# Attention in a hybrid DeltaNet and windowed-attention layer: softmax scaling moved into the transposition of the probabilities

## The chip, the cores and the metric

The kernel runs on one core of one Trainium2 chip. The core has five engines that run side by side, each working through its own queue of instructions in order: PE (TensorE, matmuls; its weight loads are shown as PEld), DVE (VectorE), ACT (ScalarE), POOL (GpSimd) and SP (SyncE, which here only issues DMAs). The metric is the time of one execution on the device in microseconds (us).

## What is computed

One layer of a diffusion backbone over 2048 latent tokens and 256 context tokens, model width 1024. One projection of the normalised, modulated input feeds two mixers: a bidirectional gated DeltaNet in chunks, and an attention over a window of |i-j| <= 128 plus all context keys. Both are gated, projected, merged by sigmoid gates and projected once more. Only the attention is touched by the change:

```python
s_loc = einsum('bnqhgd,bnkhd->bhgnqk', qb, kw) * scale      # window: 3 blocks of 128 keys
s_loc = where(valid, s_loc, NEG_INF)
s_ctx = einsum('bnqhgd,bkhd->bhgnqk', qb, kc) * scale       # 256 context keys
p = softmax(concatenate([s_loc, s_ctx, sink_l], axis=-1), axis=-1)
o = (einsum('bhgnqk,bnkhd->bnqhgd', p[..., :nloc], vw)
     + einsum('bhgnqk,bkhd->bnqhgd', p[..., nloc:nloc + nctx], vc))
```

There are 8 query heads in 2 groups of 4; each group shares one key and value head of width 64. `sink_l` is one logit per head that counts in the denominator alone. All inputs and outputs are fp32.

## The kernel before

**Stages.** The kernel works in stages that overlap at their borders: modulation and normalisation, the projections with the short convolution (up to about 640 us), the gates with the triangular solves, the DeltaNet scan with gate products beside it (about 900 to 1320 us), the attention (about 1340 to 1768 us), and the last projection (to the end). A matmul whose operands need fp32 accuracy is mostly written as three products of rounded `fp32r` parts, high by high, low by high, high by low (lines 535 to 537 for the gates, 1247 to 1249 for the projections of both branches, `pps`). The scan multiplies plain fp32 operands instead (line 1115 is one of its products).

**Attention.** It works in 32 units. A unit is one block of 128 queries (16 blocks) and one group of four heads (2 groups). Its window has three blocks of keys (two for the first and the last block) and two blocks of context keys, so a unit has five (or four) key blocks.

- `scores` (lines 926 to 941): for each of four heads two products with the window's keys (high and low part, 384 columns) and two with the context's (256 columns) into the PSUM tile `sc`; one DVE operation (line 933) adds the band mask, scales, and writes the negated scores `pr` [128 queries x 640 keys] and the row's extreme into `sm[:, h, 1]`; ACT (line 935) takes the exponential in place and sums it into `sm[:, h, 2]`. Then the denominator of all four heads at once, on 128x4 elements: DVE add (937), ACT exponential (938), DVE add, doubling and reciprocal (939 to 941) into `sm[:, h, 3]`. POOL multiplies each head's 640 probabilities by its reciprocal (943), in place. (The doubling belongs to the gate that follows, which is kept at twice its value.)
- `weighted` (lines 948 to 970): for each key block four transpositions (957) of a head's 128x128 piece into one PSUM tile `pt`; ACT rounds it to `ph` (959), DVE takes the rest `pl` (961), and PE adds both products with the values into `av` (963, 964). At the end ACT and DVE join the halves of `av` (967, 968), POOL multiplies with the gate `szb` (969), and SP stores it.

`sc` and `pt` have two buffers each in PSUM, `av` has one; `pr` and `sm` have three.

**What sets the order.** The code names operations in program order; a scheduler then simulates the queues with costs of its own and fixes each engine's order before the run. `scores` of a unit is named two units ahead of its `weighted` (`AHEAD = 2`). Beside the attention, with less priority, come the last gate products (`rps`, lines 535 to 537) and then, not before the units that they need are done (`paced`), the projections `pps` of three of four groups of 512 tokens. Each such product consists of 12 matmuls for one branch; DVE multiplies it by its gate (`ta`, `tb`, line 1258), POOL adds the two (1263). After the last unit the last projection follows in an order written out by hand.

Of the kernel before, what the change touches and what calls it, by code (L numbers as in the profile page):

```python
# [7 lines left out]
F32 = mybir.dt.float32  # L8
# [3 lines left out]
ALU = mybir.AluOpType  # L12
# [16 lines left out]
def f32(ap):  # L29
    return ap.bitcast(F32)  # L30


def hybrid(tc, ins, out, dbg=None, upto=9):
    nc = tc.nc
    V, S, G, T = nc.vector, nc.scalar, nc.gpsimd, nc.tensor
    ctx = ExitStack()
    with ctx:
        _hybrid(ctx, tc, nc, V, S, G, T, ins, out, dbg, upto)


def _hybrid(ctx, tc, nc, V, S, G, T, ins, out, dbg, upto):
# [3 lines left out]
    cst = ctx.enter_context(tc.tile_pool(name="cst", bufs=1))  # L45
# [14 lines left out]
    ident = cst.tile([128, 128], F32, name="ident")  # L60
# [2 lines left out]
    V.tensor_copy(identr, ident)  # L63

    w_in = ins["w_in"][0]
    expo = cst.tile([128, 2], F32, name="expo")
    V.memset(expo[:, 0:1], -0.5)
    V.memset(expo[:, 1:2], 0.5)

    def rsq(o, x, j=0):  # L70

        G.tensor_tensor(o, x, expo[:, j:j + 1].to_broadcast(list(x.shape)), op=ALU.pow)
# [72 lines left out]
    def psum(tag, shape, dt=F32, name=None):  # L145
        _, p, banks = pst["left" if tag in pst["left"][2] else "right"]
        return p.tile(shape, dt, name=name or tag, tag=tag, bufs=banks[tag])
# [104 lines left out]
    if True:  # L252
# [50 lines left out]
        for j in range(2):  # L303
            mps = [psum("acc" if n == 0 else "hps", [4, 512], name=f"mps{n}") for n in range(2)]
            for k in range(KT):
# [10 lines left out]
                for w in (wmh, wml):  # L316
                    for n in range(2):
                        T.matmul(mps[n], lhsT=sil4[:, k], rhs=w[:, n * 512:(n + 1) * 512],
                                 start=k == 0 and w is wmh, stop=False)
# [578 lines left out]
    def attention(pool, big, blocks, cc):  # L898
        kc, vc, sk, band = cc

        def queries(n):

            lo_b, hi_b = max(n - 1, 0), min(n + 1, NB - 1)
            nw_ = hi_b - lo_b + 1
            W = nw_ * 128
            t0 = (NCB + lo_b) * 128
            qT = pool.tile([128, 8, 128], F32R, name="qT")
            dma(f32(qT), Qsp[n])
            kw = big.tile([128, 2, 2, 384], F32R, name="kw")
            for h in range(2):  # L910
                dma(f32(kw[:, h, :, :W]), Ksp[h, :, :, t0:t0 + W].rearrange("x p t -> p x t"))
            vw = pool.tile([128, 3, 2, 128], F32R, name="vw", bufs=2)
            dma(f32(vw[:, :nw_]), Vsp[NCB + lo_b:NCB + hi_b + 1].rearrange("c p h x -> p c h x"))
            return kw, vw, qT, nw_

        def scores(n, kv, qq):
            kw, vw, qT, nw_ = qq
            W = nw_ * 128
            p = big.tile([128, 4, 640], F32, name="pr", bufs=3)
            sm = pool.tile([128, 4, 4], F32, name="sm", bufs=3)  # L920
            for h in range(4):
                ps = psum("sc", [128, 1024])
                o = 512 - W
                hd = kv * 4 + h
                q = qT[:, hd]
                T.matmul(ps[:, o:512], lhsT=q, rhs=kw[:, kv, 0, :W], start=True, stop=False)
                T.matmul(ps[:, o:512], lhsT=q, rhs=kw[:, kv, 1, :W], start=False, stop=True)
                T.matmul(ps[:, 512:768], lhsT=q, rhs=kc[:, kv, 0], start=True, stop=False)
                T.matmul(ps[:, 512:768], lhsT=q, rhs=kc[:, kv, 1], start=False, stop=True)  # L929
                s_ = p[:, h, :W + 256]  # L930
                b0 = 128 if n == 0 else 640 if n == NB - 1 else 0

                V.tensor_tensor_reduce(s_, ps[:, o:768], band[:, b0:b0 + W + 256], -0.125, sk[:, 1, hd:hd + 1],  # L933
                                       ALU.add, ALU.min, sm[:, h, 1:2])
                S.activation(s_, s_, AF.Exp, scale=-1.0, bias=sm[:, h, 1:2], accum_out=sm[:, h, 2:3])  # L935
            es = pool.tile([128, 4], F32, name="es")
            V.tensor_tensor(es, sm[:, :, 1], sk[:, 0, kv * 4:kv * 4 + 4], op=ALU.add)
            S.activation(es, es, AF.Exp)
            V.tensor_tensor(es, es, sm[:, :, 2], op=ALU.add)
            V.tensor_scalar(es, es, 2.0, None, op0=ALU.mult)  # L940
            V.reciprocal(sm[:, :, 3], es)  # L941
            for h in range(4):
                G.tensor_scalar(p[:, h, :W + 256], p[:, h, :W + 256], sm[:, h, 3:4], 1.0, op0=ALU.mult, op1=ALU.mult)  # L943
            return p

        def weighted(n, kv, qq, p):
            kw, vw, qT, nw_ = qq
            szb = pool.tile([64, 4, 128], F32, name="szb", bufs=1)
            gate = lambda t: t[n // 4][kv * 2:kv * 2 + 2, :, n % 4 * 128:n % 4 * 128 + 128].rearrange(
                "m (e d) t -> d (m e) t", e=2)  # L950
            dma(szb, gate(zbsp))
            av = psum("av", [128, 4, 128])
            nk = nw_ + NCB
            for kb in range(nk):
                pt = psum("pt", [128, 4, 128])
                for h in range(4):
                    T.transpose(pt[:, h], p[:, h, kb * 128:kb * 128 + 128], ident)  # L957
                ph = big.tile([128, 4, 128], F32R, name="ph")
                S.copy(ph, pt)  # L959
                pl = pool.tile([128, 4, 128], F32R, name="pl")  # L960
                V.tensor_tensor(pl, pt, f32(ph), op=ALU.subtract)  # L961
                v = vw[:, kb, kv] if kb < nw_ else vc[:, kb - nw_, kv]
                T.matmul(av, lhsT=v, rhs=ph, start=kb == 0, stop=False)
                last = T.matmul(av, lhsT=v, rhs=pl, start=False, stop=kb == nk - 1)
            units_done.append(last.ins)
            t = pool.tile([64, 4, 128], F32, name="avt", bufs=1)
            S.copy(t, av[64:128])
            V.tensor_tensor(t, av[0:64], t, op=ALU.add)
            G.tensor_tensor(t, t, szb, op=ALU.mult)
            dma(gate(ybsp), t)  # L970

        units = [(n, kv) for n in blocks for kv in range(2)]
        qs, pr = {}, {}

        def start(i):
            n, kv = units[i]
            if n not in qs:
                qs[n] = queries(n)
            pr[i] = scores(n, kv, qs[n])

        AHEAD = 2
        for i in range(AHEAD):
            start(i)
        for i, (n, kv) in enumerate(units):
            if i + AHEAD < len(units):
                start(i + AHEAD)
            weighted(n, kv, qs[n], pr.pop(i))
# [299 lines left out]
    ar_ = tc.tile_pool(name="attr", bufs=2, side="right", reuse_waits="tile")  # L1287
    ar = ar_.__enter__()
    attention(al, ar, [4 * gi + j for gi in (1, 2, 0, 3) for j in range(4)], att_consts(al))
    gates(list(range(BESIDE, 24)), (1, 0))  # L1290
    wp, last = [], {}
# [310 lines left out]
```

## Time and profile before

| | us |
|---|---|
| median of 3 runs | 1987.36 |
| lowest, highest | 1984.73, 1994.22 |
| the profiled execution | 1992.9 |
| its span, first to last instruction | 1991.2 |
| PE busy | 1917.4 |
| DVE, ACT, POOL busy | 1502.1, 802.6, 692.1 |

The profiled execution has a granted TensorE clock of 0.989 on average. In the profile a row such as `L957 PE MATMUL pt<-ident,pr` names the line of the code, the engine, the operation and the tiles by their names in the program. Busy time of PE counts each matmul from its start to its modelled end, and matmuls overlap, so a busy PE can still have room; what a matmul takes away from the next one is the distance of their starts.

### The profile page before, as it was taken

The numbers are of one execution on the slowest core, as the hardware profiler recorded it, in microseconds if no ns is written. First come the engines' busy times: TensorE is split into PE (matmuls) and PEld (weight loads), VectorE is DVE, ScalarE is ACT, GpSimd is POOL, SyncE is SP. The second block draws the span as 40 slices with busy tenths as digits, with TensorE's granted clock in tenths as the row PEclk, the third lists the DMA queues.
The fourth block names the chain that finished last, engine by engine and source line by source line (L and its number), as shares of the span: only waits on it lengthen the run. The fifth ranks groups of instructions, "written<-read, shape, count | busy, mean of one in ns | idle before, by whom it ended". The sixth has DMA issues, their size and how long they took to land. (4 is left out here: it accounts for less than half of the span.)

```text
span 1991.2 us, 32088 instructions
## 1 busy us (share of the span) xinstructions
PE 1917.4 (96%) x10947; PEld 1605.6 (81%) x10947; DVE 1502.1 (75%) x2869; ACT 802.6 (40%) x1994; POOL 692.1 (35%) x768
## 2 busy tenths in 40 slices
PE   7999999989999999999999999999989999999998
PEld 4888888779998787877888888788778887877786
DVE  6979766668776999999677776536686878747888
ACT  5755545554443323111222233225665656532221
POOL 2742211235542202004222234323555443420675
PEclk9999999999999999999999999999999999999999
DMA  7552226765547633528977877674455655455454
GB/s 263 173 142 87 91 89 161 195 157 175 151 134 196 170 106 116 145 89 237 230 232 225 240 212 207 178 216 146 143 176 171 185 161 164 119 173 190 141 169 135
DMA packets 387703, 333.12 MB, mean 167 GB/s; under 512 B 83992, under 2 KB 307536, under 8 KB 386900
## 3 DMA queue, kind: packets, MB, share of 16 engines
q1 hardware_dynamic: 352244, 288.60, 50.1%
q10 hardware_dynamic: 35296, 42.48, 6.1%
q8 instruction: 87, 1.43, 0.3%
q14 instruction: 76, 0.62, 0.1%
HBM read 220.28 MB, written 109.13 MB: 165 GB/s over the span
## 5 line engine op out<-in xcount | busy, mean ns | idle before, releaser
L535 PE MATMUL rps<-hh,wh 128*128 128x512 f32 x768 | 309.3, 403 | 3.7 <-DVE rt L829 2.5
L537 PE MATMUL rps<-hh,wl 128*128 128x512 f32 x768 | 307.6, 401 | 0.0
L536 PE MATMUL rps<-hl,wh 128*128 128x512 f32 x768 | 307.5, 400 | 0.0
L574 DVE SCALAR_TENSOR_TENSOR cacc<-y,cw,cacc 128x512 f32<-128x512 f32 (+1 forms) x224 | 164.0, 752 | 22.2 <-ACT cacc L572 18.3
L535 PEld LDWEIGHTS rps<-hh,wh 128*128 128x128 f32 x768 | 145.3, 189 | 39.4 <-DVE rt L829 3.3
L535 PE MATMUL lps<-hh,wh 128*128 128x512 f32 (+1 forms) x448 | 171.8, 384 | 0.3 <-ACT y L645 0.3
L536 PE MATMUL lps<-hl,wh 128*128 128x512 f32 (+1 forms) x448 | 171.5, 383 | 0.0
L537 PEld LDWEIGHTS rps<-hh,wl 128*128 128x128 f32 x768 | 145.2, 189 | 32.6
L536 PEld LDWEIGHTS rps<-hl,wh 128*128 128x128 f32 x768 | 145.5, 189 | 31.9
L537 PE MATMUL lps<-hh,wl 128*128 128x512 f32 (+1 forms) x448 | 171.0, 382 | 0.0
L961 DVE TENSOR_TENSOR pl<-pt,ph 128x512 fp32r<-128x512 f32 x156 | 105.4, 685 | 42.9 <-ACT ph L959 42.1
L959 ACT CAST ph<-pt 128x512 fp32r<-128x512 f32 x156 | 90.2, 585 | 110.2 <-PE pt L957 77.0
L827 ACT ACTIVATE rt<-rps 128x512 f32<-128x512 f32 x96 | 57.3, 597 | 185.0 <-PE rps L537 169.0
L933 DVE CUSTOM_DVE_ANT_0 pr<-sc,band,sk 128x640 f32<-128x640 f32 (+1 forms) x128 | 106.6, 862 | 32.1 <-PE sc L929 16.2
L943 POOL TENSOR_SCALAR pr<-pr,sm 128x640 f32<-128x640 f32 (+1 forms) x128 | 99.7, 802 | 56.5 <-DVE sm L941 39.3
L760 DVE TENSOR_TENSOR N<-N,btmp 128x62 f32<-128x62 f32 (+30 forms) x124 | 116.7, 941 | 3.0
L758 DVE TENSOR_TENSOR btmp<-N 128x62 f32<-128x62 f32 (+30 forms) x124 | 116.4, 939 | 3.1
L935 ACT ACTIVATE pr<-pr,sm 128x640 f32<-128x640 f32 (+1 forms) x128 | 104.0, 815 | 20.5 <-DVE sm L933 20.4
L246 DVE TENSOR_TENSOR wl<-wr,wh 128x512 fp32r<-128x512 f32 x120 | 92.4, 783 | 24.4 <-POOL wh L245 22.1
L1247 PE MATMUL pps<-yh,wph 128*128 128x512 f32 x256 | 105.6, 414 | 4.7 <-DVE tb L1258 2.5
L245 POOL TENSOR_SCALAR wh<-wr 128x512 fp32r<-128x512 f32 x72 | 48.8, 692 | 169.8 <-PE lps L536 97.1
L1248 PE MATMUL pps<-yl,wph 128*128 128x512 f32 x256 | 101.8, 399 | 0.0
(378 smaller groups left out, 5025.4 us busy)
## 6 DMA issues: line engine op xcount, KB each, us to landing
wr<-in_w_in_dram SPq DMA_DIRECT2D x120, 256.0 KB
kw<-Ksp SPq DMA_DIRECT2D x28, 384.0 KB
x<-vsp SPq DMA_DIRECT2D x36, 256.0 KB
k<-ksp SPq DMA_DIRECT2D x34, 256.0 KB
kT<-kTsp SPq DMA_DIRECT2D x34, 256.0 KB
wm<-in_w_mod_dram SPq DMA_DIRECT2D x16, 512.0 KB
xt<-in_x_dram SPq DMA_DIRECT2D x16, 512.0 KB
dtl<-Dsp SPq DMA_DIRECT2D x32, 256.0 KB
```

The source lines that it names most:

```text
L535: T.matmul(ps, lhsT=wh[:, k], rhs=xh[:, k], start=k == 0, stop=False)
L536: T.matmul(ps, lhsT=wh[:, k], rhs=xl[:, k], start=False, stop=False)
L537: T.matmul(ps, lhsT=wl[:, k], rhs=xh[:, k], start=False, stop=k == kt - 1)
L574: V.scalar_tensor_tensor(a, y[:, t:t + n], cw[:, m, t:t + 1], a, op0=ALU.mult, op1=ALU.add)
L758: V.tensor_tensor(tv, A[:, m + 1:, m].unsqueeze(2).to_broadcast([h1 + n, r, m]), A[:, m, 0:m].unsqueeze(1).to_broadcast([h1 + n, r, m]), o ...
L760: V.tensor_tensor(A[:, m + 1:, 0:m], A[:, m + 1:, 0:m], tv, op=ALU.add)
L933: V.tensor_tensor_reduce(s_, ps[:, o:768], band[:, b0:b0 + W + 256], -0.125, sk[:, 1, hd:hd + 1], ALU.add, ALU.min, sm[:, h, 1:2])
L935: S.activation(s_, s_, AF.Exp, scale=-1.0, bias=sm[:, h, 1:2], accum_out=sm[:, h, 2:3])
L943: G.tensor_scalar(p[:, h, :W + 256], p[:, h, :W + 256], sm[:, h, 3:4], 1.0, op0=ALU.mult, op1=ALU.mult)
L961: V.tensor_tensor(pl, pt, f32(ph), op=ALU.subtract)
L1247: T.matmul(ps, lhsT=wh[:, k, ms], rhs=hs[k], start=k == 0, stop=False)
L1248: T.matmul(ps, lhsT=wh[:, k, ms], rhs=ls[k], start=False, stop=False)
```

## The change

The four multiplications of the probabilities by the reciprocal disappear. In their place POOL makes, for each unit and head, a diagonal matrix `dg` of 128x128 with the factor on its diagonal (the identity multiplied by one scalar per row), and the transposition becomes an ordinary matmul of two fp32 operands: `pr` transposed times `dg`, which transposes and scales at once. The small operations of the denominator that DVE did go to POOL: two adds, and instead of doubling and reciprocal a power of -1 (by `rsq`, line 72, which raises to the exponent in a column of `expo`); the factor 0.5 is put in with the diagonal. The exponential stays on ACT. `dg` has seven buffers.

```diff
-    expo = cst.tile([128, 2], F32, name="expo")
+    expo = cst.tile([128, 3], F32, name="expo")
     V.memset(expo[:, 0:1], -0.5)
+    V.memset(expo[:, 2:3], -1.0)
     V.memset(expo[:, 1:2], 0.5)
...
             es = pool.tile([128, 4], F32, name="es")
-            V.tensor_tensor(es, sm[:, :, 1], sk[:, 0, kv * 4:kv * 4 + 4], op=ALU.add)
+            G.tensor_tensor(es, sm[:, :, 1], sk[:, 0, kv * 4:kv * 4 + 4], op=ALU.add)
             S.activation(es, es, AF.Exp)
-            V.tensor_tensor(es, es, sm[:, :, 2], op=ALU.add)
-            V.tensor_scalar(es, es, 2.0, None, op0=ALU.mult)
-            V.reciprocal(sm[:, :, 3], es)
+            G.tensor_tensor(es, es, sm[:, :, 2], op=ALU.add)
+            rsq(sm[:, :, 3], es, 2)
+            return p, sm
+
+        def weighted(n, kv, qq, pr_):
+            kw, vw, qT, nw_ = qq
+            p, sm = pr_
+            dg = []
             for h in range(4):
-                G.tensor_scalar(p[:, h, :W + 256], p[:, h, :W + 256], sm[:, h, 3:4], 1.0, op0=ALU.mult, op1=ALU.mult)
-            return p
-
-        def weighted(n, kv, qq, p):
-            kw, vw, qT, nw_ = qq
+                dg.append(pool.tile([128, 128], F32, name="dg", bufs=7))
+                G.tensor_scalar(dg[h], ident, sm[:, h, 3:4], 0.5, op0=ALU.mult, op1=ALU.mult)
...
                 for h in range(4):
-                    T.transpose(pt[:, h], p[:, h, kb * 128:kb * 128 + 128], ident)
+                    T.matmul(pt[:, h], lhsT=p[:, h, kb * 128:kb * 128 + 128], rhs=dg[h], start=True, stop=True)
```

Since the scheduler sets the order anew, instructions move within the attention; every engine's order up to the first unit's transpositions is the old one but for the added memset, and that of the last projection is too. In the changed file the lines of the attention stand three further down (the products at 960, `ph` at 962, `av` at 966 and 967, the POOL adds of the projections at 1266), the diagonals are at 950, the denominator's operations at 938 to 940, `rsq` at 73.

On PE, at the end of a unit beside the projections and the start of the next, the order was (waits behind the names: whose events an instruction waits for; x3 are three more of the same):

```order
L963 MATMUL av<-ph,vw 128x512 [waits Activation_49]
L964 MATMUL av<-pl,vw 128x512 [waits DVE_49]
L957 MATMUL pt<-ident,pr 128x128 [waits PE_49]
L957 MATMUL pt<-ident,pr 128x128 x3
L963 MATMUL av<-ph,vc 128x512 [waits Activation_49]
L964 MATMUL av<-pl,vc 128x512 [waits DVE_49]
L957 MATMUL pt<-ident,pr 128x128 [waits PE_49,Pool_49]
L957 MATMUL pt<-ident,pr 128x128 [waits Pool_49] x3
L963 MATMUL av<-ph,vc 128x512 [waits Activation_49]
```

and is now:

```order
L967 MATMUL av<-pl,vw 128x512 [waits DVE_49]
L960 MATMUL pt<-dg,pr 128x128 [waits PE_49]
L960 MATMUL pt<-dg,pr 128x128 x3
L966 MATMUL av<-ph,vc 128x512 [waits Activation_49]
L967 MATMUL av<-pl,vc 128x512 [waits DVE_49]
L960 MATMUL pt<-dg,pr 128x128 [waits PE_49,Pool_49]
L960 MATMUL pt<-dg,pr 128x128 [waits Pool_49] x3
L966 MATMUL av<-ph,vc 128x512 [waits Activation_49]
```

The first four of line 957 or 960 are the unit's last key block, the next four the first key block of the unit after it; the two value products between them are the same. What PE waits for from POOL was the scaled `pr` and is now `dg`. The scheduler also puts eight of the gate products (`rps`) that stood beside the first four units beside the fifth, and beside the later units it splits a projection's 12 matmuls in other places; each of units 8 to 31 has about the 24 that it had.

POOL's queue for two units beside the projections was:

```order
L943 TENSOR_SCALAR pr<-pr,sm 128x640 [waits DVE_49,PE_49,Activation_49]
L943 TENSOR_SCALAR pr<-pr,sm 128x640 [waits Activation_49] x3
L1263 TENSOR_TENSOR ta<-ta,tb 128x512 [waits DMAHW2_49,DVE_49,Pool_49]
L969 TENSOR_TENSOR avt<-avt,szb 64x512 [waits DMAHW3_49,DMAHW2_49,DVE_49]
L943 TENSOR_SCALAR pr<-pr,sm 128x640 [waits DVE_49,PE_49,Activation_49]
L943 TENSOR_SCALAR pr<-pr,sm 128x640 [waits Activation_49] x3
L1263 TENSOR_TENSOR ta<-ta,tb 128x512 [waits DMAHW0_49,DVE_49]
L969 TENSOR_TENSOR avt<-avt,szb 64x512 [waits DMAHW2_49,DMAHW1_49,DVE_49]
```

and for one unit it is now:

```order
L938 TENSOR_TENSOR es<-sm,sk 128x4 [waits DVE_49]
L972 TENSOR_TENSOR avt<-avt,szb 64x512 [waits DMAHW1_49,DMAHW0_49,DVE_49]
L940 TENSOR_TENSOR es<-es,sm 128x4 [waits Activation_49]
L73 TENSOR_TENSOR sm<-es,expo 128x4 [waits Pool_49]
L950 TENSOR_SCALAR dg<-ident,sm 128x128 [waits PE_49]
L1266 TENSOR_TENSOR ta<-ta,tb 128x512 [waits DMAHW2_49,DVE_49]
L950 TENSOR_SCALAR dg<-ident,sm 128x128 [waits PE_49,Pool_49]
L950 TENSOR_SCALAR dg<-ident,sm 128x128 [waits PE_49] x2
```

The single diagonal ahead of `ta` is the fourth of one unit; the three behind it are the first three of the unit after. Each waits for PE to be done with the buffer that it writes.

## The prediction

> **What bounds the kernel now.** I read the busy table of the page first, then the costliest groups that the change touches (line, engine, operation, out<-in, shape, count | busy us, mean ns of one | idle before it, and who ended it).
>
> ```profile
> PE 1917.4 (96%) x10947; PEld 1605.6 (81%) x10947; DVE 1502.1 (75%) x2869; ACT 802.6 (40%) x1994; POOL 692.1 (35%) x768
> ```
>
> ```profile
> L943 POOL TENSOR_SCALAR pr<-pr,sm 128x640 f32<-128x640 f32 (+1 forms) x128 | 99.7, 802 | 56.5 <-DVE sm L941 39.3 <-PE av L963 4.9 <-PE sc L929 3.9
> L957 PE MATMUL pt<-ident,pr 128*128 128x128 f32 x624 | 92.8, 273 | 0.0
> ```
>
> POOL's scaling is a large group on an engine that is 35% busy; the transpositions never had PE idle ahead of them (0.0). PE's 96% is an average, and its matmuls overlap, so next I cut the attention into three stretches: the gates beside the first units, four units with nothing beside them, the remaining 24 units with the projections; the fourth row is what follows. Columns: stretch, length, busy us and count of PE, PEld, DVE, ACT, POOL, granted clock, DMA share, GB/s.
>
> ```profile
> 1357.30:1422.70 65.40, 65.40 (x356) 55.86 (x355) 38.73 (x90) 35.20 (x78) 22.27 (x28) 1.00 0.40 129
> 1422.70:1464.10 41.40, 34.40 (x186) 25.99 (x185) 33.93 (x77) 33.07 (x74) 28.40 (x28) 1.00 0.62 196
> 1464.10:1767.80 303.70, 295.21 (x1606) 248.17 (x1605) 224.86 (x469) 169.78 (x365) 138.72 (x143) 0.99 0.51 156
> 1767.80:1991.20 223.40, 205.87 (x866) 163.54 (x864) 172.50 (x191) 52.90 (x78) 99.85 (x63) 0.97 0.52 167
> ```
>
> In the first stretch PE is never idle. In the second, DVE is busy 82% and PE 83%: nobody alone sets the pace. The third decides, being the longest. There I take starts instead of busy time, since a matmul's start after the one before it is what PE really spends on it. Timeline of one unit, columns start, duration, line, shape, count:
>
> ```profile
> 1625.36 0.39 PE L1249 MATMUL pps<-yh,wpl 128*128 128x512 f32 x1
> 1625.59 0.60 PE L957 MATMUL pt<-ident,pr 128*128 128x128 f32 x4
> ...
> 1626.62 0.33 PE L926 MATMUL sc<-kw,qT 128*128 128x384 f32 x1
> 1626.79 0.33 PE L927 MATMUL sc<-kw,qT 128*128 128x384 f32 x1
> 1626.96 0.28 PE L928 MATMUL sc<-kc,qT 128*128 128x256 f32 x1
> 1627.08 0.27 PE L929 MATMUL sc<-kc,qT 128*128 128x256 f32 x1
> ```
>
> 512 columns cost 0.23 us (1625.59 - 1625.36), 384 cost 0.17, 256 cost 0.12. Four transpositions span 0.60 and one lasts 0.273 (its group's mean), so they start (0.60 - 0.27)/3 = 0.109 apart and a group of four costs 0.44. What the third stretch issues:
>
> ```profile
> L1247 PE MATMUL pps<-yh,wph 128*128 128x512 f32 x192 | 80.1, 417 | 2.3 <-ACT yh L1227 2.3
> ...
> L957 PE MATMUL pt<-ident,pr 128*128 128x128 f32 x460 | 68.9, 273 | 0.0
> L926 PE MATMUL sc<-kw,qT 128*128 128x384 f32 (+1 forms) x84 | 31.6, 376 | 2.2 <-DVE sm L933 2.2
> ...
> L963 PE MATMUL av<-ph,vw 128*128 128x512 f32 x68 | 27.2, 401 | 0.2 <-ACT ph L959 0.2
> ...
> L928 PE MATMUL sc<-kc,qT 128*128 128x256 f32 x85 | 24.0, 282 | 0.0
> L963 PE MATMUL av<-ph,vc 128*128 128x512 f32 x48 | 22.8, 474 | 3.4 <-ACT ph L959 3.4
> ```
>
> L1247 has two companions of the same count, and L926, L928 and L963 one each. So 3x192 + 2x(68 + 48) = 808 products of 512 columns at 0.233 are 188.3 us, 168 at 0.17 are 28.6, 170 at 0.12 are 20.4, 460 transpositions at 0.109 are 50.1: 287.4 of 303.7. **PE has 16.3 us left in 24 units, 0.7 us in each: this stretch is bound by PE's issue.** A unit of the second stretch issues 20 transpositions, 10 of 512, 8 of 384 and 8 of 256 columns: 6.8 us, four of them 27.3 of 41.4, so 14.1 us are free.
>
> **What the change costs, part by part.** *The products on PE.* `T.transpose` becomes `T.matmul` on two fp32 operands. An fp32 product of this shape stands in the scan:
>
> ```profile
> 1007.00 1.06 PE L1115 MATMUL vps<-x,mx 128*128 128x128 f32 x8
> 1007.89 0.27 PE L1027 MATMUL mtp<-ident,mx 128*128 128x128 f32 x1
> ```
>
> Line 1115 issues four products, and the trace has eight records: two for each product, against one for a transposition (624 are 156 groups of four). The eight take 0.89 us to PE's next start. So a group of four rises from 0.44 to 0.89, by 0.45 us, and 156 groups by 70.2. By stretch: 84 transpositions in the first (21 groups, 9.5 us), 80 in the second (20 groups, 9.0), 460 in the third (115 groups, 51.8).
>
> Third stretch: of 51.8 at most 16.3 fall into the gaps that are left. The gaps come from these waits (who <- whom: us in total, times, longest us):
>
> ```profile
> PEld av L963 <- ACT ph L959: 4.6, 4, 2.4
> PEld sc L926 <- DVE sm L933: 4.1, 10, 1.5
> ...
> PEld pps L1247 <- ACT yh L1227: 3.0, 3, 1.9
> ```
>
> A wait gets shorter only where the awaited work runs on while PE is at its longer products. `ph` and `sm` are made from PE's own results (pt, sc) and move along with it; only the split of a loaded `yh` does not. I take that 3.0 as filled: 48.8, with bounds 35.5 and 51.8. First stretch: no gap, +9.5, but the new order carries eight gate products of 0.23 into the fifth unit, -1.9: +7.6 (bounds 7.6 and 9.5). Second stretch: 9.0 and those 1.9 go into 14.1 free us, while DVE is relieved as below: 0, with bounds -4.3 (DVE's relief passed on in full) and +9.0 (nothing hidden).
>
> *Work that leaves DVE.*
>
> ```profile
> L937 DVE TENSOR_TENSOR es<-sm,sk 128x4 f32<-128x4 f32 x32 | 16.0, 499 | 0.1
> ...
> L939 DVE TENSOR_TENSOR es<-es,sm 128x4 f32<-128x4 f32 x32 | 6.7, 208 | 4.9 <-ACT es L938 4.4
> L940 DVE TENSOR_SCALAR es<-es 128x4 f32<-128x4 f32 x32 | 5.9, 185 | 1.0
> L941 DVE RECIPROCAL sm<-es 128x4 f32<-128x4 f32 x32 | 5.7, 179 | 0.9
> ```
>
> 34.3 us, 1.07 per unit. In the third stretch DVE is 74% busy, so this is worth nothing there; in the second it is at most 4 x 1.07 = 4.3, the bound above.
>
> *POOL.* It loses 99.7 us. It gains 64 small adds, 32 powers and 128 diagonals:
>
> ```profile
> L943 POOL TENSOR_SCALAR pr<-pr,sm 128x640 f32<-128x640 f32 x112 | 88.9, 816 | 50.5 <-DVE sm L941 35.9 <-PE av L963 4.9 <-PE sc L929 3.9
> L72 POOL TENSOR_TENSOR ssn<-ssn,expo 128x4 f32<-128x4 f32 x41 | 49.1, 1197 | 36.4 <-DVE ssn L403 30.3 <-DVE ssn L438 4.7
> ...
> L969 POOL TENSOR_TENSOR avt<-avt,szb 64x512 f32<-64x512 f32 x32 | 41.7, 1303 | 108.6 <-DVE avt L968 64.7 <-DVE es L937 37.0 <-issue 6.9
> ...
> L1067 POOL TENSOR_TENSOR fss<-fss,al 128x4 f32<-128x4 f32 x16 | 3.7, 234 | 31.8 <-ACT fjunk L1066 31.8
> ...
> L1068 POOL TENSOR_SCALAR fss<-fss 128x4 f32<-128x4 f32 x16 | 3.6, 224 | 1.4
> ```
>
> An add is 0.23, a power 1.2. A 128x128 diagonal lies between 0.22 (4 columns) and 0.82 (640 columns); on the straight line between them it is 0.34, which I take. Together 15.0 + 38.3 + 43.5 = 96.8 us (81 to 158 with the ends): POOL is as busy as before and still far from full, 139 of 304 us in the third stretch. What is hidden here is hidden by the lookahead: scores of a unit are issued two units ahead, 25 us in the third stretch (2 x 303.7/24), and the chain of add, exponential (row below: lowest, median and highest ns), add, power and diagonal is 0.23 + 0.20 + 0.23 + 1.2 + 0.34 = 2.2 us. Without that cover it would cost 2.2 us a unit, 70 in all.
>
> ```profile
> L938 ACT ACTIVATE es<-es x32: 190/202/210, 1352.8 to 1742.3; 128x4 f32<-128x4 f32 x32
> ```
>
> *A new wait.* `dg` has seven buffers, so a unit's fourth diagonal waits for head 0 of the last products of the unit before. In the new order two value products (2 x 0.23) stand between these groups. Counted from the start of that last group, the buffer is free at 0.22 + 0.16 (a matmul's 0.27 less its 0.11 to the next start) = 0.4, and the diagonal is ready at about 0.8; PE asks for it at 0.89 + 0.46 + 3 x 0.22 = 2.0. It is hidden by 1.2 us as long as POOL is free at that moment. Queued behind it on POOL are `ta`, the next three diagonals and the next `es`, none of them due within a unit. SP's and ACT's DMA issues keep their number, and the extra memset of `expo` lies at the start, under the first loads.
>
> *The clock.* The granted clock is 1.00 in the second stretch, where transpositions are 8.7 of 27.3 us, and 0.99 in the third: nothing here says that they lower it. The Trainium skill's TensorE: Matmul & The Clock Gate, Part 4 (PE-mode transpose), says that a transposition does not count as activity for the clock gate; by it products would lift the 0.99, worth at most 3 us of 303.7, a sum of 53 instead of 56. The trace's 1.00 in the densest stretch does not bear it out.
>
> **Sum:** 48.8 + 7.6 + 0 = +56 us; between the bounds +39 and +70. The profiled execution took 1992.9 us with a span of 1991.2 and would become 2049; it is 5.5 above the median of the runs, 1987.4, so the predicted median is **2043 us**.
>
> **Rivals.** *The gaps take more* (0.13): the scheduler fills every gap of the three stretches, and the sum is its lower bound, +39: 2026. For it: 30 us of gaps. Against it: 0.7 us a unit is made of waits of fractions of a microsecond.
> *Diagonals too late* (0.15): POOL is inside `avt` (1.3) and a power (1.2) when the buffer comes free, and PE stands before the fourth head. It decides once more than 1.2 us are queued; 2.5 would cost PE up to 1.3 a unit, half of it in 32 units 21 us: 2064. Against it: `avt` and the power are due several us earlier in the unit.
> *Not slower* (0.04): PE is not the pace; units go by the chain denominators, POOL, transpositions, and PE's share is cover. Then 70 us hide, and the second stretch gives back DVE's 4.3: 1983. It decides if more than 2.25 us of each unit are free on PE. For it: POOL waits 39.3 us for `sm`. Against it: 0.7, and no PE idle ahead of L957.
> *Four passes at the transposition's price* (0.01): 4 x 0.109 for a product, +0.327 in 624 of them, +204: 2191. The scan's 0.89 for four speaks against it. The Trainium skill's FP8 and Floating Point Precision, TensorE Precision Notes, counts four passes for true fp32; by that row two records of 0.111 hold them.
>
> **Chances.** The forecast has 0.67. A time within 0.5% (10 us, about what a measurement of this kernel can tell from no change) or a faster one comes only out of the third rival: faster 0.03, same 0.01, slower 0.96. For 8 in 10 the range takes in the bounds, 2026 to 2058, the late diagonals, and a few us of scatter (the runs span 1984.7 to 1994.2): 2022 to 2066.
>
> **What would show it.** The products' line with 1248 records, its groups of four 0.89 us from start to start; the third stretch about 49 us longer and the second as long as now; POOL's busy total within a few us of 692. If PE idles ahead of the products on POOL's `dg`, the second rival holds; if the records are 624, or a group costs 0.44, the price was wrong; if stretch three grows by under 36, the gaps were not what I took them for.

## The result, and the profile after

| | before | after |
|---|---|---|
| median, us | 1988.08 | 2056.2 |
| lowest, highest | 1984.73, 1994.22 | 2054.16, 2061.31 |
| the profiled execution | 1992.9 | 2061.3 |
| its span | 1991.2 | 2059.6 |

The changed kernel takes 1.0345 times as long (95% interval 1.0325 to 1.0365), 68 us more. The forecast was 2043, with 2022 to 2066 as its range: slower, as predicted, and within the range, but 13 us above the forecast.

The busy table of the changed kernel, and from its groups the products and, for the attention's time (1340 to 1850), POOL's new work:

```profile
PE 1976.4 (96%) x11571; PEld 1676.0 (81%) x11571; DVE 1480.8 (72%) x2742; ACT 804.4 (39%) x1994; POOL 684.3 (33%) x864
```

```profile
L960 PE MATMUL pt<-dg,pr 128*128 128x128 f32 x1248 | 165.7, 275 | 0.9 <-POOL dg L950 0.7
```

```profile
L950 POOL TENSOR_SCALAR dg<-ident,sm 128x128 f32<-128x128 f32 x128 | 47.1, 384 | 108.2 <-PE pt L960 107.7
...
L73 POOL TENSOR_TENSOR sm<-es,expo 128x4 f32<-128x4 f32 x32 | 33.3, 1041 | 2.4
...
L938 POOL TENSOR_TENSOR es<-sm,sk 128x4 f32<-128x4 f32 x32 | 7.7, 241 | 118.8 <-DVE sm L934 113.3 <-DMA yr<-yasp 5.4
L940 POOL TENSOR_TENSOR es<-es,sm 128x4 f32<-128x4 f32 x32 | 6.7, 211 | 5.1 <-ACT es L939 5.0
```

PE has 624 instructions more, 1248 products' records where 624 transpositions stood. POOL's new work is 47.1 + 33.3 + 7.7 + 6.7 = 94.8 us against the 99.7 that left. PE idled 0.7 us in all ahead of the products for a diagonal.

PE's timeline of a stretch beside the projections shows the price (start, duration):

```profile
1656.55 1.05 PE L960 MATMUL pt<-dg,pr 128*128 128x128 f32 x8
1657.36 0.42 PE L927 MATMUL sc<-kw,qT 128*128 128x384 f32 x1
1657.62 0.34 PE L928 MATMUL sc<-kw,qT 128*128 128x384 f32 x1
...
1665.31 1.05 PE L960 MATMUL pt<-dg,pr 128*128 128x128 f32 x8
1666.12 0.48 PE L966 MATMUL av<-ph,vc 128*128 128x512 f32 x1
```

Eight records last 1.05 us, one lasts 0.275: they start (1.05 - 0.275)/7 = 0.111 apart, and a group of four takes 8 x 0.111 = 0.89. (The row behind such a group starts after 0.81 already, but lasts 0.42 where its kind lasts 0.34: the 0.08 are in it.)

The same four stretches as before (first units beside gates; units alone; units beside projections; what follows), with the same columns. In the table below them, `start` is how much later the first stretch begins (1359.0 against 1357.3):

```profile
1359.00:1431.20 72.20, 72.20 (x431) 64.31 (x430) 36.85 (x71) 36.15 (x79) 21.09 (x41) 1.00 0.36 113
1431.20:1476.50 45.30, 42.30 (x276) 36.93 (x275) 30.79 (x60) 33.42 (x72) 27.09 (x40) 1.00 0.60 180
1476.50:1821.10 344.60, 340.55 (x2066) 302.14 (x2064) 206.27 (x383) 172.36 (x367) 134.03 (x210) 1.00 0.46 139
1821.10:2059.60 238.50, 208.04 (x866) 163.77 (x865) 173.04 (x190) 51.36 (x76) 99.53 (x63) 0.96 0.49 156
```

| | start | first | second | third | rest | sum |
|---|---|---|---|---|---|---|
| predicted, us | 0 | +7.6 | 0 | +48.8 | 0 | +56 |
| measured, us | +1.7 | +6.8 | +3.9 | +40.9 | +15.1 | +68.4 |

So 48 of the 68 us came in the two stretches where they were expected, somewhat less than was predicted; 4 came in the second stretch, and 15 after the attention, where the prediction had nothing. In that last stretch PE is busy 208.0 us (205.9 before) and idle 30.5 (17.5 before): it does the same work and waits longer. ACT's timeline, with the loads that its queue issues, shows where (start, duration; in brackets idle time before it and who ended it):

```profile
1832.11 1.23 ACT L1230 CAST yh<-yr 128x512 fp32r<-128x512 f32 x2 [7.00 <-DMA yr<-ybsp]
...
1859.36 0.43 ACTq L1339 DMA_DIRECT2D B<-in_w_out_dram  x1
...
1877.59 1.90 ACT L1383 CAST B11h<-B 128x2048 fp32r<-128x2048 f32 x1 [44.25 <-DMA B<-in_w_out_dram]
```

In the kernel before, the first two of these instructions stood 0.6 us apart, and the third came 7 us after them:

```profile
1779.76 1.24 ACT L1227 CAST yh<-yr 128x512 fp32r<-128x512 f32 x2 [5.01 <-DMA yr<-ybsp]
1780.39 0.43 ACTq L1336 DMA_DIRECT2D B<-in_w_out_dram  x1
...
1787.48 1.91 ACT L1380 CAST B11h<-B 128x2048 fp32r<-128x2048 f32 x1 [6.47 <-issue]
```

The load of the first output weights `B`, which the last projection needs, is issued 27 us after the last split of `yh` instead of 0.6 us. The split of these weights (`B11h`), behind all four loads in ACT's queue, comes 45.5 us after it instead of 7.7. What the first load waits for is seen in ACT's order, here its row before and after (waits in brackets, as in the orders above):

```
L1336 DMA B<-in_w_out_dram 128x4x512
L1339 DMA B<-in_w_out_dram 128x4x512 [waits DMAHW3_49,DVE_49,Pool_49]
```

The trace has such a wait in ACT's queue, 9.5 us long up to the issue; before there was none:

```profile
L1339 ACTq EVENT_SEMAPHORE  x1: 9537/9537/9537, 1849.8 to 1849.8; - x1
```

On DVE's timeline a sum of the projections ends at 1858.60 + 0.69 = 1859.29, just before the issue at 1859.36:

```profile
1858.60 0.69 DVE L1266 TENSOR_TENSOR ta<-ta,tb 128x512 f32<-128x512 f32 x1
```

It is the last sum but two; those two (line 1279, from 1891.6 on) take their `tb` from another pool. So the load waited, by these times, until the projections' own pool had its `tb` read for the last time. Nothing in the changed lines names `B` or `tb`.

### The profile page after: what moved, and what is told of

Read it like the earlier page. It is cut to its first block, busy times and chain, and to the rows that moved or that the text cites. A ratio compares the mean times of both kernels' runs of the same rounds, so it can differ in the third digit from the quotient of the medians.

```text
span 2059.6 us, 33388 instructions
## 1 busy us (share of the span) xinstructions
PE 1976.4 (96%) x11571; PEld 1676.0 (81%) x11571; DVE 1480.8 (72%) x2742; ACT 804.4 (39%) x1994; POOL 684.3 (33%) x864
## 5 line engine op out<-in xcount | busy, mean ns | idle before, releaser
L575 DVE SCALAR_TENSOR_TENSOR cacc<-y,cw,cacc 128x512 f32<-128x512 f32 (+1 forms) x224 | 163.5, 751 | 22.0 <-ACT cacc L573 17.9
L960 PEld LDWEIGHTS pt<-dg,pr 128*128 128x128 f32 x1248 | 162.6, 191 | 11.8 <-POOL dg L950 1.0
L960 PE MATMUL pt<-dg,pr 128*128 128x128 f32 x1248 | 165.7, 275 | 0.9 <-POOL dg L950 0.7
```

The source lines that it names most:

```text
L575: V.scalar_tensor_tensor(a, y[:, t:t + n], cw[:, m, t:t + 1], a, op0=ALU.mult, op1=ALU.add)
L960: T.matmul(pt[:, h], lhsT=p[:, h, kb * 128:kb * 128 + 128], rhs=dg[h], start=True, stop=True)
```

## Experiments

Two theories were open at the start. The 15 us at the end: either **placement** (the seven diagonals, 512 bytes a partition each, push later tiles of the pool along, and `B` comes to lie where `tb` is still in use), or a consequence of the attention's **new order and timing**. The attention's 53 us: either **PE's records alone**, or a part from POOL's and DVE's new duties. All ratios are to the kernel before, timed on the same chip.

### A block of the diagonals' size, and nothing else

```diff
+        pad = pool.tile([128, 7, 128], F32, name="pad", bufs=1)
+        G.memset(pad[:, 0, 0:1], 0.0)
         units = ...
```

> The kernel before, with nothing changed but one unused tile of 7 x 128 fp32 columns in the attention's left pool, where the changed kernel keeps its diagonals. Theory (of the 68 us, some 15 are no work at all: the diagonals' memory pushes later tiles so that the first load of the output weights has to wait for a tile that is still in use): the attention as before, the part after it about 15 us longer, 2003 us. Rival (the part after the attention got longer because the attention hands it its results in another rhythm): no change, 1988.

Measured: 2005.3 us (2002.4 to 2006.0), ratio 1.0074 (1.0047 to 1.0101), +17.5 us. Its last stretch is as long as that of the changed kernel, with the attention as before (65.4, 42.2 and 302.8 us), and its load of `B` stands 28 us behind the last `yh`, right behind the end of the same sum (1804.34 + 0.69 = 1805.03):

```profile
1765.90:2004.30 238.40, 209.26 (x866) 164.99 (x864) 172.34 (x191) 52.65 (x78) 99.83 (x63) 0.95 0.49 156
```

```profile
1777.42 1.23 ACT L1229 CAST yh<-yr 128x512 fp32r<-128x512 f32 x2 [5.19 <-DMA yr<-ybsp]
...
1805.11 0.43 ACTq L1338 DMA_DIRECT2D B<-in_w_out_dram  x1
```

It is placement. Neither products, nor diagonals, nor a new order are needed for these 15 us.

### The diagonals in the other pool

The attention has two pools, one at either end of the memory. The same seven buffers, taken from the other one:

```diff
-                dg.append(pool.tile([128, 128], F32, name="dg", bufs=7))
+                dg.append(big.tile([128, 128], F32, name="dg", bufs=7))
```

> The changed kernel, with the diagonals in the attention's other pool. Theory (placement): the load of the output weights waits for nothing again, 15 us less than the changed kernel, 2041 us. Rival (the rhythm): as the changed kernel, 2056.

Measured: 2039.08 us (2037.7 to 2039.8), ratio 1.0245 (1.0212 to 1.0277): 17 us less than the changed kernel, from one word. The third stretch stays, the last one is short again:

```profile
1471.80:1815.60 343.80, 340.47 (x2066) 302.22 (x2064) 205.82 (x383) 172.55 (x367) 133.30 (x210) 1.00 0.46 139
1815.60:2037.40 221.80, 204.57 (x865) 162.29 (x865) 172.38 (x190) 51.65 (x76) 99.50 (x63) 0.99 0.52 168
```

Its first load of `B` is issued at 1827.3, 33 us ahead of that sum (1860.4), and no longer waits for it. The two experiments answer each other: the block alone makes the loss, moving the block away removes it. What is left, +51 us, is the attention.

### The products alone

The kernel before, its scaling on POOL and its denominator on DVE kept, with a product by the plain identity in place of each transposition:

```diff
-                    T.transpose(pt[:, h], p[:, h, kb * 128:kb * 128 + 128], ident)
+                    T.matmul(pt[:, h], lhsT=p[:, h, kb * 128:kb * 128 + 128], rhs=ident, start=True, stop=True)
```

> The kernel before, with the transposition alone replaced by an fp32 product with the identity; scaling stays on POOL and the denominators on DVE. Theory (PE's issue is the price): all of the attention's loss is here, +53 us, 2041. Rival (the diagonals, their buffers and the denominators on POOL cost a good part): at most +30, 2018 or less.

Measured: 2042.88 us (2041.3 to 2051.3), ratio 1.0274 (1.024 to 1.0308), +55 us.

```profile
1429.70:1477.20 47.50, 41.93 (x275) 36.93 (x274) 36.08 (x76) 33.57 (x72) 28.61 (x28) 1.00 0.57 178
1477.20:1820.40 343.20, 339.29 (x2067) 302.44 (x2066) 225.28 (x471) 171.93 (x367) 138.97 (x143) 1.00 0.45 139
```

The third stretch is that of the changed kernel within 1.4 us: all of its loss is the products. In the second stretch DVE still makes its denominators, and it is 47.5 us long against 44.6 with the diagonals in the other pool. Whether these 3 us are DVE's relief is not shown by this run alone, since POOL's work and the order differ too.

### The denominator's operations alone

```diff
-            V.tensor_tensor(es, sm[:, :, 1], sk[:, 0, kv * 4:kv * 4 + 4], op=ALU.add)
+            G.tensor_tensor(es, sm[:, :, 1], sk[:, 0, kv * 4:kv * 4 + 4], op=ALU.add)
             S.activation(es, es, AF.Exp)
-            V.tensor_tensor(es, es, sm[:, :, 2], op=ALU.add)
-            V.tensor_scalar(es, es, 2.0, None, op0=ALU.mult)
-            V.reciprocal(sm[:, :, 3], es)
+            G.tensor_tensor(es, es, sm[:, :, 2], op=ALU.add)
+            rsq(sm[:, :, 3], es, 2)
```

The transposition and POOL's four multiplications stay, with the factor 0.5 in the latter; `expo` has its third column as in the change.

> The kernel before, with the denominator's small operations alone on POOL (two adds and the power; the factor 0.5 goes into the scaling); transpositions and scaling stay. Theory: 34 us leave DVE where it sets no pace, so 0 to -4, 1984 to 1988. Rival (the longer chain over POOL makes PE wait for the scaled probabilities): +10 to +30, 1998 to 2018.

Measured: 1986.98 us (1984.3 to 1995.6), ratio 0.9992 (0.9974 to 1.0009). No change that can be measured. The second and the third stretch:

```profile
1425.20:1470.90 45.70, 37.60 (x186) 29.40 (x185) 32.61 (x61) 33.53 (x74) 31.29 (x39) 0.89 0.57 178
1470.90:1772.30 301.40, 294.65 (x1606) 248.21 (x1605) 202.41 (x381) 167.53 (x363) 171.30 (x209) 0.99 0.51 157
```

DVE has 22 us less than before in the third stretch, POOL 33 us more, and the stretch is 2.3 us shorter. Neither engine sets the pace there. The second stretch, with as many PE records as before (186), did not get shorter by DVE's relief: 45.7 us, at a granted clock of 0.89, against 41.4 at 1.00.

### No scaling at all

The kernel before without POOL's four multiplications:

```diff
-            for h in range(4):
-                G.tensor_scalar(p[:, h, :W + 256], p[:, h, :W + 256], sm[:, h, 3:4], 1.0, op0=ALU.mult, op1=ALU.mult)
```

> The kernel before, with POOL's multiplication of the probabilities left out (the output lacks the softmax's denominator); transpositions, denominators and all else stay. Theory (POOL is hidden): 0 to -4, 1984 to 1988. Rival (units go by the chain through POOL, so that removing its 100 us could have paid for the products): -30, 1958.

Measured: 1990.31 us (1984.7 to 1994.6), ratio 1.0001 (0.9985 to 1.0018). The third stretch has POOL at half of its work and is as long as ever:

```profile
1461.10:1765.30 304.20, 298.15 (x1606) 249.53 (x1605) 224.38 (x469) 170.46 (x365) 71.44 (x55) 0.99 0.51 157
```

The multiplications that the change removes cost nothing in the first place, so nothing could be won by removing them.

### Two transpositions instead of one

Is it the fp32 product that is dear, or any second pass over the piece? The kernel before, each transposition done twice into the same place:

```diff
-                    T.transpose(pt[:, h], p[:, h, kb * 128:kb * 128 + 128], ident)
+                    for _ in range(2):
+                        T.transpose(pt[:, h], p[:, h, kb * 128:kb * 128 + 128], ident)
```

> The kernel before, with each of the 624 transpositions issued twice into the same place. Theory (PE's issue, whatever the instruction): a group of four goes from 0.44 to 0.87 us, nearly the 0.89 of the products, so +51, 2039. Rival (fp32 products cost by their weight loads of 0.19 us, which a transposition with 0.14 does not have): clearly less, +25, 2013.

Measured: 2044.1 us (2041.75 to 2050.7), ratio 1.0289 (1.0261 to 1.0317), +55 us, as with the products. Its third stretch, and its weight loads (lowest, median and highest ns, which for the products are 186, 192 and 192):

```profile
1473.90:1819.10 345.20, 341.08 (x2067) 297.77 (x2065) 223.68 (x471) 171.89 (x367) 138.99 (x143) 1.00 0.45 138
```

```profile
L958 PEld LDWEIGHTS pt<-ident,pr x1248: 137/140/231, 1354.0 to 1814.8; 128*128 128x128 f32 x179
```

A shorter weight load makes no difference to the end. What is paid is the issue of a second record for each piece. The Trainium skill's Perfetto Trace Analysis, Optimizing Tensor Performance, advises the transposition instead of an ordinary matmul for transposing; this trace agrees, with 0.44 against 0.89 us for four pieces.

### Four and six buffers for the diagonals

On top of the diagonals in the other pool, `bufs=7` becomes `bufs=4`, so that a unit's diagonals each wait for the same head of the unit before:

> The changed kernel with the diagonals in the other pool and four buffers instead of seven, so that each of the four, not the fourth alone, waits for the products of the unit before. Theory: the first is ready 0.8 us after the start of that last group and the others 0.38 apart, PE asks at 1.35 and 0.22 apart: still hidden, by 0.1 to 0.5 us, 2041 to 2045. Rival (late diagonals): PE stands before each unit for 0.5 to 1.3 us, 2057 to 2080.

Measured: 2057.47 us (2049.8 to 2059.2), ratio 1.0338 (1.0312 to 1.0364), 68.1 us over the kernel before, where seven buffers in the same place had 51.2. This expectation missed: I had taken nearly all of the later diagonals to be covered. The time is that of the rival, but not by the rival's path, as the waits below show. The third stretch:

```profile
1478.00:1832.40 354.40, 347.80 (x2067) 304.88 (x2065) 206.71 (x384) 172.20 (x367) 136.92 (x213) 1.00 0.44 135
```

It is 10.6 us longer than with seven, 0.44 us for each of 24 units. The waits in the whole attention (who <- whom: us in total, times, longest), first with four buffers, then with seven:

```profile
POOL dg L950 <- PE pt L960: 131.1, 27, 7.3
...
PEld av L966 <- ACT ph L962: 9.6, 16, 2.1
...
PEld sc L927 <- DVE sm L934: 3.6, 11, 0.9
...
PEld pt L960 <- POOL dg L950: 1.8, 3, 1.0
```

```profile
POOL dg L950 <- PE pt L960: 108.1, 27, 7.4
...
PEld av L966 <- ACT ph L962: 4.5, 7, 1.5
...
PEld sc L927 <- DVE sm L934: 1.2, 4, 0.7
...
PEld pt L960 <- POOL dg L950: 1.0, 1, 1.0
```

POOL is held 23 us more by the buffers, but PE itself waits only 0.8 us more for a diagonal; its waits for `ph` and `sm` grow by 5.1 and 2.4. So PE does not stand before the diagonals. The scheduler also orders PE's work differently for four buffers, and this run does not separate that from the later diagonals. Six buffers:

> The changed kernel with the diagonals in the other pool and six buffers, so that the third and the fourth wait for the products of the unit before. With seven it took 2039, with four 2057. Theory (POOL is held by each diagonal that has to wait, and the rest of its queue with it, so the time grows with the number that wait): between them, 2042 to 2050. Rival (four is slow by another cause, such as the order that the scheduler made for it): as with seven, 2037 to 2041.

Measured: 2047.06 us (2046.3 to 2048.1), ratio 1.0288 (1.027 to 1.0306), between the two.

```profile
1471.20:1819.90 348.70, 343.69 (x2067) 305.31 (x2065) 205.60 (x383) 171.62 (x367) 135.76 (x211) 0.99 0.45 137
1819.90:2045.30 225.40, 205.39 (x866) 161.87 (x865) 172.29 (x190) 51.74 (x76) 99.55 (x63) 0.99 0.51 165
```

So fewer buffers cost time, step by step; by which path the loss reaches PE at six and four stays open. No run has more than seven, so whether seven still cost something is not shown; PE waits 1.0 us for a diagonal there.

No version that was run beats the kernel before.

## Why the prediction was right, and where it was off

**The mechanism and the price: right.** Two records a product, 1248 in all, 0.89 us a group. The products alone cost +55 us in the runs, where the change as a whole, without its placement, costs +51 (the two intervals overlap).

**The remainder of the program: wrong, 0 against +15.1.** This is the step that failed. The prediction took the last projection as unchanged because its order was the old one. The rows were the same, but not what they wait for: the list of waits behind the first load of `B` had three entries more, and that stood in the order before the run. I compared rows there and not waits. The block alone gives +15.0 in this stretch (238.4 against 223.4), the other pool takes it away. The load came 27 us late, but PE had the projections' last products to do meanwhile, and idled 11.0 us ahead of the last projection's first product, for `ah`, which ACT makes behind `B11h`:

```profile
L1484 PE MATMUL P<-B11h,ah 128*128 128x512 f32 x32 | 13.7, 427 | 11.0 <-ACT ah L1366 11.0
```

In all, PE's idle time is 12.9 us longer in this stretch (ahead of the products that read a new `ah` 15.2 against 3.2), and its busy time 2.2: that is the 15.1. The granted clock is 0.81 in the 45 us from the pause on, against 0.96 in 45 us of the kernel before where its last projection begins (1815 to 1860 us); whether the pause brings this with it was not tested by itself.

```profile
1868.30:1913.30 45.00, 28.60 (x101) 20.78 (x100) 32.17 (x31) 16.86 (x17) 0.00 (x0) 0.81 0.44 152
```

**Third stretch: mis-sized, +48.8 against +40.9**, within its bounds of 35.5 and 51.8. The products' 51.8 are there: 188.3 + 28.6 + 20.4, and 920 records at 0.111 = 102.1, make 339.4 of 344.6. So 5.2 us are free where 16.3 were; the gaps took 11.1, not 3.0. (Both sums count 32 products of 256 columns, inside the group of line 926 and its companion, at the price of 384. Put right, 6.8 us are free where 17.9 were, with the same difference.) The step that failed is the one that let `ph` and `sm` move along with PE. With PE at its longer groups, DVE and ACT catch up: in the third stretch the weight loads' waits for `sm` fell from 4.1 us to 0.5, those for `ph` from 4.6 to 3.3, those for `pl` from 1.5 to 0.5, and those for `yh`, the one term taken as filled, from 3.0 to 0.5. Together that is 8.4 of the 11.1 us; the rest is not pinned down.

```profile
PEld av L966 <- ACT ph L962: 3.3, 2, 1.8
...
PEld pt L960 <- POOL dg L950: 1.0, 1, 1.0
...
PEld av L967 <- DVE pl L964: 0.5, 1, 0.5
PEld pps L1250 <- ACT yh L1230: 0.5, 1, 0.5
PEld sc L927 <- DVE sm L934: 0.5, 2, 0.3
```

It is the longer PE work that covers them and not DVE's relief: with the products alone, where DVE keeps its denominators, the stretch is as short (343.2) and the wait for `sm` is gone too, while with the denominators alone on POOL it stays at 4.1.

**Second stretch: 0 against +3.9**, within -4.3 and +9.0. The step that failed is the one that put 9.0 and 1.9 us wholly into the 14.1 free ones: PE's busy time grew from 34.4 to 42.3 of 45.3, and the stretch with it. With the products alone it is +6.1, and with the transpositions doubled +6.3 (47.7 against 41.4); in these runs too the gate products have moved in (275 records of PE, of which 80 are new by the products or the doubling, against 186). So products and gate products cost about 6 us here, and the whole change 2 to 3 less. DVE's relief is the likely reason, but not shown: the run with the relief alone has no gain in this stretch.

**First stretch: +7.6 against +6.8.** No gap, and the gate products that moved into the fifth unit: right.

**POOL: right.** 94.8 us against an estimate of 96.8: the adds 0.24 and 0.21 (0.23), the power 1.04 (1.2), the diagonal 0.37 to 0.38 (0.34). The fourth diagonal's wait is hidden with seven buffers, as worked out: one wait of 1.0 us in the third stretch. The rival *diagonals too late* does not hold here. With four buffers the time came near its 2064 (2057), but PE waited only 1.8 us for diagonals there, so its path is not confirmed.

**The other rivals.** *The gaps take more* was in part true in the third stretch, and far from it in the second. *Not slower* and *four passes at the transposition's price* are out: the 24 units that decide had about 0.7 us free each, not 2.25, without the scaling on POOL the kernel is no faster, and a group took 0.89 us.

**The clock.** The third stretch went from 0.99 to 1.00. With the block alone, its transpositions untouched, it has 1.00 as well, with the transpositions doubled also 1.00, and with products and six buffers 0.99. The Trainium skill's TensorE: Matmul & The Clock Gate, Part 4, says that transpositions do not count as activity for the clock gate; these runs do not bear that out, nor can differences of 0.01 decide it.

**The sum of the errors.** +15.1 (placement), +3.9 (second stretch), +1.7 (the attention's start, which in the profiles of the experiments lies anywhere from 1346.5 to 1360.0), -0.8 and -7.9: 12 of the 13 us. That 2056 still lies in the range is partly luck. The range went up to 2066 for late diagonals, which did not come; placement, which no rival named, took that room, and the third stretch's smaller loss made up for half of it.

## What to carry to other kernels

Price an edit on the engine that sets the pace by its records' start-to-start distance, and what it saves elsewhere by the cover that lies over it: here 100 us of POOL's work and 34 of DVE's were worth next to nothing beside 55 us of PE's. When a tile is added, compare what later instructions wait for, not only their order: a few kilobytes in a pool (3.5 a partition here) can put a load behind a tile that is still in use, far away from the edit. Where two engines exchange work through a unit's chain, gaps on the busiest engine shrink when it gets more to do, but not to nothing: here by some three fifths (11.1 of 17.9 us).

## What was not expected of the hardware

- The weight loads of an fp32 product take 192 ns against 140 for a transposition, and yet a product and two transpositions cost the kernel the same (+55 us each): the loads lie beside the matmuls (302 us of loads beside 339 of matmuls in the 343 us of the third stretch, with the products alone).
- A power on 128x4 elements on POOL took 1.04 us in the attention, four to five times an add of the same size (0.21 to 0.24).
- A load that came 27 or 28 us late cost its stage 15 us, in the changed kernel and with the block alone. With four or six buffers in the other pool, where no load came late in this way, the stage was 225.1 and 225.4 us long against 221.8 with seven, which no run explains.
